# Low parts of the first MLP product's weights in blocks 1 to 3: a subtraction on VectorE replaced by a negated copy and an adding DMA

## The chip, the cores and the metric

One Trainium2 chip, one of its cores. The program runs on that core alone. The metric is the device time of one execution in microseconds: the median of three runs before the change is 722.54 us (721.73 to 723.35).

## What is computed

One layer of a decoder trunk on a sequence of 512 tokens of width 1024, all in float32: a norm, three token mixers side by side (stick-breaking attention, causal pooling, chunked gating), an output projection, and then a dense MLP with squared ReLU. The change concerns the MLP alone. Cut to it, the reference is:

```python
h = rms_norm(x, g_ff_pre[l])
ff = jnp.square(jax.nn.relu(h @ w_ff_in[l])) @ w_ff_out[l]
x = x + rms_norm(ff, g_ff_post[l])
```

`h` is 512x1024, `w_ff_in` 1024x4096, `w_ff_out` 4096x1024.

## The kernel before

**Split products.** Every float32 operand of a matmul is split into two float32r tiles, a high part `hi` (the value copied to float32r) and a low part `lo` (the value less `hi`). A product of two split operands is three matmuls, high by high, high by low and low by high (`mm3`, line 265). In the first MLP product the order on TensorE is weights' high by activations' high, weights' high by activations' low, weights' low by activations' high, so that the low part of the weights is wanted third in each k-step.

**Weights.** All weight matrices pass through one plan of chunks (`plan`, lines 112 to 175), each 128 partitions by 1024 values, 512 KB. `load_chunk` (line 179) issues the load of the next chunk on SP into one of three `raw` buffers. `split_chunk` (line 188) makes `whi` and `wlo`, of which there are six each: a copy on ScalarE into `whi`, and a subtraction raw minus `whi` on VectorE into `wlo`. Then it issues the load of the next chunk, which takes the raw buffer that is free first. A chunk of the first MLP product is four k-tiles of 256 columns, so that each of its 512 rows is 1 KB in memory. `Weights.ready` (line 243) makes chunks up to three ahead of the one in use (`AHEAD`), as far as six buffers allow.

**The MLP.** It runs in four blocks (`b`, line 949) of 1024 hidden columns. Each block has the first product, eight tiles `f` of 128 hidden columns (`ff_in`, line 874; 8 k-steps of three matmuls each), and the second product in four stages, `s2`, `s1`, `s3`, `s4` (lines 1010 to 1068), a scheme of half-size products in which VectorE also forms sums of weight blocks (`block_sums`, line 217). The first product of a block uses eight chunks, in pairs: the first of a pair has the first four k-steps, the second the other four, and both serve two tiles `f`. So the second chunk of a pair is wanted first four k-steps after the first. `ff_act` (line 890) takes each finished tile from PSUM, applies ReLU and square on ScalarE, forms sums on VectorE and splits them, for the second product only.

**Order.** TensorE and SP keep the order of the program (`InOrder`, line 80). For ScalarE and VectorE that order is switched off in the MLP (line 971), and the compiler's scheduler orders them by its own estimate. In the MLP after the first block's beginning, POOL has no work until the norm at the end.

Of the kernel before, what the change touches and what calls it, by code (L numbers as in the profile page):

```python
# [13 lines left out]
AF = mybir.ActivationFunctionType  # L14
ALU = mybir.AluOpType
# [33 lines left out]
def trunk_layer(ctx: ExitStack, tc: tile.TileContext, x, w_in, w_pool, pool_scale, gm_gain,  # L49
                w_spatial, b_spatial, w_br_sb, w_br_pool, w_br_gm, w_out, g_mix_pre,  # L50
                g_mix_post, g_ff_pre, g_ff_post, w_ff_in, w_ff_out, out):
    nc = tc.nc
# [45 lines left out]
    pe, act, dve, sp = (InOrder(e, True) for e in (nc.tensor, nc.scalar, nc.vector, nc.sync))  # L98
# [13 lines left out]
    plan = []  # L112

    derive = {}

    def plan_cols(w, c0, n=256):

        first = len(plan)
        for k in range(0, w.shape[1], CHUNK // n):
            plan.append([w[:, k:k + CHUNK // n, c0:c0 + n]])  # L120
        return range(first, len(plan))

    use = {}
    use["v"] = plan_cols(w_in_k, C_V, 512)

    def plan_qk(hp):
# [3 lines left out]

    plan_qk(0)
    use["u"] = plan_cols(w_in_k, C_U)
    use["gv"] = plan_cols(w_in_k, C_GV)
    plan_qk(1)
    use["p"] = plan_cols(w_in_k, C_P)
# [24 lines left out]
    for b in range(NB):  # L160
        for f in range(0, FT, 2):
            use["f1", b, f] = plan_cols(ff_in_k, (b * FT + f) * P)


        for stage in ("s2", "s1", "s3", "s4"):
            use[stage, b] = range(len(plan), len(plan) + (2 if stage == "s2" else FT // 2))
            for m in range(0, FT // 2, 2 if stage == "s2" else 1):
                b11, b12, b21, b22 = (
                    ff_out_k[:, b * FT + 2 * m + o:b * FT + 2 * m + o + 1, c:c + 512]
                    for o in range(2) for c in (0, 512))  # L170
                if stage == "s2":
                    plan.append([ff_out_k[:, b * FT + 2 * m + 1:b * FT + 2 * m + 4:2, :512]])
                else:
                    plan.append({"s1": [b11, b12], "s3": [b22, b12], "s4": [b22, b21]}[stage])
                    derive[len(plan) - 1] = (stage, m)

    loaded, made = [], []

    def load_chunk():
        raw = wp.tile([P, CHUNK], F32, name="raw", bufs=RAW)  # L180
        at = 0
        for v in plan[len(loaded)]:
            _, a, b = v.shape
            sp.dma_start(raw[:, at:at + a * b].rearrange("p (a b) -> p a b", a=a), v)
            at += a * b
        loaded.append(raw)

    def split_chunk(engines="v"):
        raw = loaded[len(made)]
        hi = wp.tile([P, CHUNK], F32R, name="whi", bufs=HL)  # L190
        lo = wp.tile([P, CHUNK], F32R, name="wlo", bufs=HL)
        if len(made) in derive:
            pieces = block_sums(raw, *derive[len(made)])
        else:
            pieces = [raw[:, n * CHUNK // len(engines):(n + 1) * CHUNK // len(engines)]
                      for n in range(len(engines))]
        at = 0
        for n, piece in enumerate(pieces):
            c = slice(at, at + piece.shape[1])
            at = c.stop  # L200
            e = engines[n % len(engines)]
            act.copy(hi[:, c], piece)
            (nc.gpsimd if e == "p" else dve).tensor_sub(lo[:, c], piece, hi[:, c].bitcast(F32))
        at = 0
        outs = []
        for v in plan[len(made)]:
            _, a, b = v.shape
            outs.append(tuple(t[:, at:at + a * b].rearrange("p (a b) -> p a b", a=a)
                              for t in (hi, lo)))
            at += a * b  # L210
        made.append(outs)
        if len(loaded) < len(plan):
            load_chunk()
# [3 lines left out]
    def block_sums(raw, stage, m):  # L217

        one, two = raw[:, :512], raw[:, 512:]
        if stage == "s1":  # L220
            t1s[m] = ff.tile([P, T], F32, name="t1", bufs=4)
            dve.tensor_add(t1s[m], one, two)
            return [one, t1s[m]]
        if stage == "s3":

            dve.tensor_add(t1s[m], t1s[m], one)
            dve.tensor_add(two, two, one)
            return [t1s[m], two]
        dve.tensor_add(two, two, t1s[m])
        return [raw]  # L230

    class Weights:
# [10 lines left out]
        def ready(self, i):  # L243
            live = self.chunks.start if self.keep else i
            while len(made) < min(len(plan), i + 1 + self.ahead, live + HL):
                split_chunk()
# [124 lines left out]
    if True:  # L371
# [32 lines left out]
        for step in V_ORDER.split():  # L404
            what = step.rstrip("0123")
            t, g = ([int(c) for c in step[len(what):]] + [0, 0])[:2]
            if what == "sq":
                if g == 0:
                    two[t] = sm.tile([P, 2], F32, name="n2")
                square_sum(xts[t][g], two[t][:, g:g + 1])  # L410
            elif what == "rms":
                rs[t] = rstd_d(two[t], "n")
            elif what == "scale":
                hns[t, g] = scaled(xts[t], rs[t], gpre, g)
            elif what == "turn":
                pts[t, g] = transposed(hns[t, g], bank("z", "trx"))
            elif what == "cols":
                split_to(hT, pts[t, g], t, g)
            elif what.startswith("split"):
                split_chunk(what[len("split"):])  # L420
            else:
                for which in {"hh": (0,), "rest": (1,), "mm": (0, 1)}[what]:
                    v_part(t, g, which)
# [432 lines left out]
    def between(t, k):  # L856

        if k == 2 and t >= 2:
            turn(t - 2)
        if k == 2 and t == 3:  # L860
            split_chunk("pp")
            later["ssq"] = residual(2, later["r"])
# [235 lines left out]
```

## Time and profile before

| | |
|---|---|
| runs, us | 721.73, 723.35, 722.54 |
| the profiled execution's own time, us | 722.87 |
| its span, first to last instruction, us | 721.1 |
| granted TensorE clock over the span | 0.996 of full speed |
| first products of blocks 1, 2 and 3, us from the span's start | 464.4 to 507.9, 546.15 to 589.7, 628 to 671.5 |
| DMA traffic | 89.80 MB, mean 125 GB/s |

The span counts from the first to the last instruction of one profiled execution; its own time includes what lies around it. A stage is named by the stretch of the span in which TensorE works on it. TensorE's matmuls are pipelined: one begins every 0.227 us, though each is shown as 0.39 us long.

### The profile page before, as it was taken

How to read it: one execution, taken by the hardware profiler on the slowest of the kernel's cores; microseconds unless marked ns; L12 is line 12 of the kernel's file. 1: busy time of each engine (PE TensorE's matmuls, PEld its weight loads, DVE VectorE, ACT ScalarE, POOL GpSimd, SP SyncE). 2: the span in 40 equal slices, each digit the busy share in tenths (PEclk: the TensorE clock that was granted, in tenths of full speed). 3: DMA queues.
4: the chain of work that ended last, by engine and by line, in shares of the span. 5: the costliest groups of instructions: out<-in, count | busy, mean ns of one | idle time of the engine just before them, and what ended most of it. 6: DMA issues, size and time to landing. Idle time of an engine off the chain costs nothing.

```text
span 721.1 us, 9135 instructions
## 1 busy us (share of the span) xinstructions
PE 698.6 (97%) x3320; PEld 576.7 (80%) x3320; DVE 494.0 (68%) x771; ACT 353.9 (49%) x593; POOL 54.0 (7%) x106
## 2 busy tenths in 40 slices
PE   7999999999999999999999998999999999999994
PEld 4889887788888888888889777888888888888774
DVE  6745799777777544243576776747885679757897
ACT  6566666655444333321445654555534553445541
POOL 4100222111121000000040000000000000000001
PEclk9999999999999999999999999999999999999998
DMA  8272312322325233262325235633356234643543
GB/s 278 80 207 84 115 60 60 90 68 70 96 59 146 89 90 114 74 220 87 116 89 176 99 106 175 181 113 115 119 165 208 92 117 148 188 133 116 162 160 117
DMA packets 72432, 89.80 MB, mean 125 GB/s; under 512 B 4546, under 2 KB 49730, under 8 KB 72387
## 3 DMA queue, kind: packets, MB, share of 16 engines
q1 hardware_dynamic: 72384, 89.21, 39.5%
q8 instruction: 26, 0.43, 0.2%
q14 instruction: 20, 0.16, 0.1%
q10 hardware_dynamic: 2, 0.00, 0.0%
HBM read 85.01 MB, written 4.19 MB: 124 GB/s over the span
## 4 chain that ended last, share of the span: by engine, by line
PE 80%; DVE 10%; DMA 4%; ACT 3%; issue 2%; POOL 1%; SPq 0%; POOLq 0%; DVEq 0%; ACTq 0%
PE psc L90 25%; PE accf L90 18%; PE accx L90 7%; PE psb L90 6%; PE acc L90 6%; PE accz L90 5%; PE accy L90 4%; PE psv L90 3%; DMA raw<-in_w_ff_out_dram 3%; DVE wlo L90 2%; DVE ys L90 2%; PE psgv L90 2%; PE z L90 1%; PE av L90 1%; PE pt L90 1%
## 5 line engine op out<-in xcount | busy, mean ns | idle before, releaser
L90 DVE TENSOR_TENSOR wlo<-raw,whi 128x1024 fp32r<-128x1024 f32 (+1 forms) x145 | 158.1, 1095 | 109.6 <-ACT whi L90 108.8
L90 ACT CAST whi<-raw 128x1024 fp32r<-128x1024 f32 (+1 forms) x152 | 139.4, 927 | 140.5 <-PE psc L90 31.0
L90 PE MATMUL psc<-hT,whi 128*128 128x512 f32 x576 | 182.2, 398 | 0.0
L90 PE MATMUL accf<-hT,whi 128*128 128x512 f32 x448 | 138.1, 390 | 1.4 <-ACT rl L90 1.4
L90 PEld LDWEIGHTS psc<-hT,whi 128*128 128x128 f32 x576 | 103.9, 188 | 21.0 <-issue 1.5
L90 PE MATMUL psc<-hT,wlo 128*128 128x512 f32 x288 | 112.6, 391 | 0.0
L90 PEld LDWEIGHTS accf<-hT,whi 128*128 128x128 f32 x448 | 84.0, 188 | 19.1 <-ACT rl L90 1.8
L90 PE MATMUL accf<-hT,wlo 128*128 128x512 f32 x224 | 87.2, 389 | 0.0
L90 PEld LDWEIGHTS psc<-hT,wlo 128*128 128x128 f32 x288 | 54.1, 188 | 11.6
L90 PEld LDWEIGHTS accf<-hT,wlo 128*128 128x128 f32 x224 | 42.1, 188 | 8.8
L90 ACT CAST ah<-ec 128x768 fp32r<-128x768 f32 (+1 forms) x32 | 30.2, 944 | 32.6 <-DVE ec L90 32.1
L90 PE MATMUL accx<-whi,ah 128*128 128x512 f32 x96 | 37.9, 394 | 2.9 <-DVE ys L90 2.9
L284 POOL TENSOR_TENSOR pr<-pv,mhalf 128x1 f32<-128x1 f32 x8 | 4.8, 605 | 470.7 <-DVE pv L90 470.7
L90 DVE TENSOR_TENSOR al<-ec,ah 128x768 fp32r<-128x768 f32 (+1 forms) x32 | 34.8, 1087 | 4.7 <-ACT ah L90 4.5
L90 PE MATMUL accx<-wlo,ah 128*128 128x512 f32 x96 | 37.4, 390 | 0.0
L90 PE MATMUL accx<-whi,al 128*128 128x512 f32 x96 | 37.4, 390 | 0.0
L90 DVE TENSOR_TENSOR_SCAN nb<-nb,zeros 128x128 f32<-128x128 f32 (+3 forms) x32 | 27.5, 863 | 7.5 <-POOL nb L482 7.1
L90 DVE TENSOR_TENSOR ec<-ec 128x256 f32<-128x256 f32 x64 | 26.7, 421 | 7.0 <-ACT ec L90 6.7
L90 ACT CAST whi<-t 128x512 fp32r<-128x512 f32 x32 | 19.7, 616 | 14.8 <-DVE t L90 9.2
L90 PE MATMUL accy<-whi,al 128*128 128x512 f32 (+1 forms) x64 | 24.7, 386 | 1.9 <-DVE al L90 1.9
L90 ACT CAST a<-pt 128x128 fp32r<-128x128 f32 (+3 forms) x32 | 13.6, 426 | 25.9 <-PE pt L90 25.8
L90 ACT ACTIVATE sg<-psc 128x512 f32<-128x512 f32 x24 | 14.3, 598 | 22.7 <-PE psc L90 22.7
(197 smaller groups left out, 1236.0 us busy)
## 6 DMA issues: line engine op xcount, KB each, us to landing
raw<-in_w_ff_out_dram SPq DMA_DIRECT2D x96, 256.0 KB, 3.2
raw<-in_w_in_dram SPq DMA_DIRECT2D x42, 512.0 KB, 3.8
raw<-in_w_ff_in_dram SPq DMA_DIRECT2D x32, 512.0 KB, 3.9
xt<-in_x_dram SPq DMA_DIRECT2D x16, 256.0 KB, 6.3
raw<-in_w_out_dram SPq DMA_DIRECT2D x8, 512.0 KB, 3.7
raw<-in_w_ff_out_dram SPq DMA_DIRECT2D x8, 512.0 KB, 3.8
raw<-in_w_br_sb_dram SPq DMA_DIRECT2D x4, 512.0 KB, 3.4
x1d<-xt SPq DMA_DIRECT2D x8, 256.0 KB, 2.7
```

The costliest lines, as they stand in the source:

```text
L90: i = op(*args, **kw).ins
L284: nc.gpsimd.tensor_tensor(r, v, mhalf, ALU.pow)
```

## The change

For the chunks of the first MLP product in blocks 1, 2 and 3 (`summed`, 8 chunks in each, 24 in all), `split_chunk` makes the low part in another way. ScalarE copies raw into `whi`, as before, and then copies raw times -1 into `wlo`. GpSimd's queue (POOL) then issues a DMA that reads the same chunk of `w_ff_in` from memory once more and adds it to what stands in `wlo`. VectorE has no part in these chunks. Block 0 and all other weights are made as before.

```diff
+    summed = set()
+
...
             use["f1", b, f] = plan_cols(ff_in_k, (b * FT + f) * P)
+            if b:
+                summed.update(use["f1", b, f])
...
         hi = wp.tile([P, CHUNK], F32R, name="whi", bufs=HL)
         lo = wp.tile([P, CHUNK], F32R, name="wlo", bufs=HL)
-        if len(made) in derive:
+        if len(made) in summed:
+            act.copy(hi, raw)
+            act.activation(lo, raw, AF.Copy, scale=-1.0)
+            v, = plan[len(made)]
+            _, a, b = v.shape
+            nc.gpsimd.dma_start(lo.rearrange("p (a b) -> p a b", a=a), v, accum_op=ALU.add)
+            pieces = []
+        elif len(made) in derive:
             pieces = block_sums(raw, *derive[len(made)])
```

How the instructions stand. On ScalarE at the head of block 1, in the last stage of block 0's second product (`ys` is the running output, `whi` and `wlo` the parts of weight chunks, `rl` and `ec` the ReLU and square of the first finished tile), the kernel before has:

```order
L90 CAST whi<-raw 128x1024
L90 ACTIVATE ys<-accx 128x512
L90 CAST whi<-raw 128x1024 x2
L90 ACTIVATE ys<-accx 128x512
L90 CAST whi<-raw 128x1024 x5
L90 ACTIVATE rl<-accf 128x512
```

and the changed one has, in the same place:

```order
L90 CAST whi<-raw 128x1024
L90 ACTIVATE ys<-accx 128x512
L90 CAST whi<-raw 128x1024 x2
L90 ACTIVATE wlo<-raw 128x1024
L90 ACTIVATE ys<-accx 128x512
L90 CAST whi<-raw 128x1024
L90 ACTIVATE wlo<-raw 128x1024
L90 CAST whi<-raw 128x1024
L90 ACTIVATE wlo<-raw 128x1024
L90 CAST whi<-raw 128x1024
L90 ACTIVATE wlo<-raw 128x1024
L90 CAST whi<-raw 128x1024
```

The second of the pair of CASTs is the first chunk of block 1; each first-product chunk now has a negated copy behind its CAST.

On VectorE at the same place (`accx`, `accy` and `accz` are PSUM tiles of the second product, `al` the low part of the activation sums), before:

```order
L90 TENSOR_TENSOR ys<-ys,accx 128x512
L90 TENSOR_TENSOR wlo<-raw,whi 128x1024 x5
L90 TENSOR_TENSOR ys<-ys,accz 128x512 x2
L90 TENSOR_TENSOR wlo<-raw,whi 128x1024
L90 TENSOR_TENSOR ys<-ys,accy 128x512 x2
L90 TENSOR_TENSOR wlo<-raw,whi 128x1024
L90 TENSOR_TENSOR ec<-ec 128x256
L90 TENSOR_TENSOR wlo<-raw,whi 128x1024 x2
L90 TENSOR_TENSOR ec<-ec 128x256 x2
L90 TENSOR_TENSOR al<-ec,ah 128x768
```

and after:

```order
L90 TENSOR_TENSOR ys<-ys,accx 128x512
L90 TENSOR_TENSOR wlo<-raw,whi 128x1024
L90 TENSOR_TENSOR ys<-ys,accz 128x512 x2
L90 TENSOR_TENSOR ys<-ys,accy 128x512 x2
L90 TENSOR_TENSOR ec<-ec 128x256 x3
L90 TENSOR_TENSOR al<-ec,ah 128x768
```

Eight subtractions are gone between these rows (four of the five, and the four behind them); the rest keeps its order.

On POOL, from the last norm before the MLP (`nr`) to the norms at the end (`pr`), the changed kernel has:

```order
L295 TENSOR_TENSOR pr<-pv,mhalf 128x1
L295 TENSOR_TENSOR nr<-nv,mhalf 128x1
L201 DMA wlo<-in_w_ff_in_dram 128x4x256 x24
L295 TENSOR_TENSOR pr<-pv,mhalf 128x1 x4
L1105 UNCONDITIONAL_BRANCH
```

The row of 24 transfers is new; before, the four `pr` stood right behind `nr`. TensorE's and SP's rows are the same in both kernels.

## Rows read from the trace of the kernel before

**Rows 1.** The page: span, and busy us (share) x instructions of each engine.

```profile
span 721.1 us, 9135 instructions
PE 698.6 (97%) x3320; PEld 576.7 (80%) x3320; DVE 494.0 (68%) x771; ACT 353.9 (49%) x593; POOL 54.0 (7%) x106
```

**Rows 2.** Stages: from:to, length, busy us of PE, PEld, DVE, ACT, POOL; clock; DMA.

```profile
546.15:589.70 43.55, 43.55 (x193) 36.09 (x193) 27.89 (x41) 23.05 (x33) 0.00 (x0) 1.00 0.37 122
...
671.50:690.00 18.50, 18.16 (x80) 14.72 (x80) 16.47 (x28) 9.78 (x18) 0.00 (x0) 1.00 0.62 213
690.00:721.00 31.00, 20.75 (x102) 16.99 (x100) 24.56 (x46) 8.63 (x18) 2.16 (x4) 0.91 0.28 106
```

**Rows 3.** PE's waits from 400 us: total us, times, longest.

```profile
PE accx L90 <- DVE ys L90: 2.9, 2, 2.0
PE accy L90 <- DVE al L90: 1.9, 2, 1.6
PE accf L90 <- ACT rl L90: 1.4, 1, 1.4
```

**Rows 4.** Timeline, last block, PE and DVE: start, length, engine, work [idle before].

```profile
694.85 0.50 PE L90 MATMUL accx<-whi,ah 128*128 128x512 f32 x1 [0.98 <-DVE ys L90]
...
674.82 0.69 DVE L90 TENSOR_TENSOR t<-t,raw 128x512 f32<-128x512 f32 x1 [1.58 <-DMA raw<-in_w_ff_out_dram]
```

**Rows 5.** Instruction groups from 380 us: count | busy us, mean ns | idle before.

```profile
L90 DVE TENSOR_TENSOR wlo<-raw,whi 128x1024 fp32r<-128x1024 f32 x52 | 63.2, 1222 | 35.8 <-ACT whi L90 35.6
L90 ACT CAST whi<-raw 128x1024 fp32r<-128x1024 f32 x52 | 54.1, 1051 | 78.1 <-DMA raw<-in_w_ff_in_dram 20.6 <-PE accf L90 17.4 <-PE accx L90 16.9
```

**Rows 6.** Timeline of ACT at the heads of blocks 1, 2 and 3.

```profile
453.00 1.99 ACT L90 CAST whi<-raw 128x1024 fp32r<-128x1024 f32 x2
...
457.69 1.05 ACT L90 CAST whi<-raw 128x1024 fp32r<-128x1024 f32 x1 [2.21 <-DMA raw<-in_w_ff_in_dram]
...
533.31 2.95 ACT L90 CAST whi<-raw 128x1024 fp32r<-128x1024 f32 x3 [4.61 <-PE accx L90]
539.48 1.05 ACT L90 CAST whi<-raw 128x1024 fp32r<-128x1024 f32 x1 [3.22 <-DMA raw<-in_w_ff_in_dram]
...
615.12 2.95 ACT L90 CAST whi<-raw 128x1024 fp32r<-128x1024 f32 x3 [4.65 <-PE accx L90]
621.24 1.05 ACT L90 CAST whi<-raw 128x1024 fp32r<-128x1024 f32 x1 [3.17 <-DMA raw<-in_w_ff_in_dram]
```

**Rows 7.** Timeline of PE: low-part matmuls at the heads of blocks 1, 2 and 3.

```profile
464.68 0.39 PE L90 MATMUL accf<-hT,wlo 128*128 128x512 f32 x1
...
546.44 0.39 PE L90 MATMUL accf<-hT,wlo 128*128 128x512 f32 x1
...
549.16 0.39 PE L90 MATMUL accf<-hT,wlo 128*128 128x512 f32 x1
...
628.25 0.39 PE L90 MATMUL accf<-hT,wlo 128*128 128x512 f32 x1
```

**Rows 8.** Loads of first-product chunks: SP issue, ns min/median/max; time to landing.

```profile
L90 SPq DMA_DIRECT2D raw<-in_w_ff_in_dram x32: 367/368/384, 328.6 to 630.0; - x32
...
DMA to landing us min/median/max: 3.6/3.9/5.2
```

**Rows 9.** DMA busy tenths and GB/s, 538 to 543 us, in 40 slices.

```profile
DMA  9999994179114992699999999999999999997238
GB/s 385 393 393 377 360 361 156 33 131 74 41 25 49 106 90 57 205 344 385 369 393 393 369 377 385 377 377 393 393 393 377 385 393 385 385 369 254 74 57 147
```

**Rows 10.** Stages of 5 us at the head of block 2; last columns DMA share, GB/s.

```profile
538.00:543.00 5.00, 5.00 (x23) 4.15 (x23) 2.31 (x2) 2.10 (x2) 0.00 (x0) 1.00 0.86 275
543.00:548.00 5.00, 5.00 (x23) 4.13 (x23) 4.87 (x6) 2.10 (x2) 0.00 (x0) 1.00 0.80 223
548.00:553.00 5.00, 5.00 (x23) 4.13 (x22) 2.42 (x4) 2.28 (x3) 0.00 (x0) 1.00 0.81 248
```

**Rows 11.** Chain of waits, 360 to 380 us: start, length, engine and work.

```profile
369.56 3.00 POOL wlo L203 x2
```

## The prediction

> **What bounds the kernel now.** I read the page's busy times first. TensorE (PE) is busy 698.6 of 721.1 us, VectorE (DVE) 494.0, ScalarE (ACT) 353.9 [rows 1]. So the reader should ask only one thing of any part of the change: does PE start a matmul sooner or later. Next I cut the span into stages. In the first product of the third MLP block (546.15 to 589.70 us) PE is busy all 43.55 us; only in the last stages, from 671.5 us on, does it have gaps [rows 2]. The waits of PE from 400 us to the end confirm it: three kinds, 2.9, 1.9 and 1.4 us, none of them on the weights of the first product [rows 3]. Of the gaps that DVE causes, the one behind the last changed block is 0.98 us, at 694.85 us [rows 4]. In the stages that the change touches there is nothing to win: PE has no gap there that a faster DVE could close.
>
> **What the change removes.** In blocks 1 to 3 it takes 24 subtractions of 128x1024 from DVE, at 1222 ns each, 29.3 us in all [rows 5]. They lie beside matmuls, so the gain on the path is 0. A gain later, through DVE's queue, would have to be carried from about 640 us to the crowded stretch from 671.5 us on, and it is not: at 674.82 us DVE stands idle for 1.58 us, waiting for a load of second-product weights [rows 4]. What DVE saves before that point is spent in such waits. I count 0.
>
> **What it adds on ACT.** 24 negated copies of 128x1024. No row shows this instruction; the nearest is the CAST of the same tile, 1051 ns [rows 5]. In a stage of 43.55 us ACT works 23.05 us [rows 2]; eight more copies make it 31.5. That fits, and the squared-ReLU work that they push back by a microsecond feeds only the second product or a PSUM bank that has a second one beside it. Cost by itself: 0. But each copy stands ahead of the adding transfer in the chain that makes a low part, so it counts below.
>
> **What it adds on POOL and the DMA engines.** 24 adding transfers of 512 KB. The low part that DVE made 1.2 us after its CAST now comes out of: CAST, negated copy, transfer. The question is whether it lands before PE wants it. POOL's queue has nothing else between the output projection and the last norm, and no load waits in it, so nothing is queued behind a transfer but the next one. SP's loads free their raw buffer at the end of the second ACT pass instead of DVE's, at about the same time (541.6 against 541.8 us for the second chunk, by rows 6 and the 1222 ns).
>
> **The windows.** In the middle of a stage a chunk has some 16 us of cover: PE uses one in 5.44 us (43.55 us for eight [rows 2]) and the code makes them three ahead. At the head of a block it has far less. There the buffers come free only as the block before ends, and the raw chunks arrive one after another. Take the second boundary. The CAST of the first chunk is the third of a group that ends at 533.31 + 2.95 = 536.26; with one more copy 537.31 [rows 6]. PE's first matmul on its low part is at 546.44 [rows 7]: window 9.1 us. The second chunk's CAST starts at 539.48; with both passes it is through at 541.58; PE wants its low part at 549.16, four k-steps of 0.68 us after the first one's: window 7.6 us. The same at the other two boundaries: first chunk 456.04 to 464.68 (8.6) and 619.12 to 628.25 (9.1); second chunk 459.79 to 464.68 + 2.72 = 467.40 and 623.34 to 630.97 (7.6 each) [rows 6, 7]. The third chunk is wanted only 10.88 us after the first, when the burst of loads is over. So PE is held at each of three boundaries by the second chunk, for what the transfer takes beyond 7.6 us.
>
> **The price of an adding transfer.** No row shows one. The nearest is the plain load of the same chunk: 3.6 to 5.2 us from issue to landing, 3.9 in the middle [rows 8]. At their busiest the engines move 393 GB/s of such loads [rows 9], so 512 KB (0.524 MB) move in 1.33 us and 2.6 us of the 3.9 are fixed.
> - Low end: it costs as much as that load, 3.9 us. It can't be below, since it moves the same bytes from the same tensor and more.
> - Passes: the sum needs the bytes of the weights and the bytes already in the tile; two passes of 1.33 us, or three if the write back counts too (2.7 or 4.0 us). The Trainium skill, "Collectives: The Full Stack", section "The bandwidth ceiling: the fold count and why AG ≠ RS ≠ AR", says that an add in the DMA engines costs by its two source reads and not by the arithmetic; by that rule two passes, and no run here shows it.
> - Sharing: from 538 to 553 us the engines are 86, 80 and 81% busy with the raw loads [rows 10]. A transfer that takes turns with them needs about twice its own time: 5.3 us for two passes, 8.0 for three.
> - POOL's part: an SP issue takes 0.37 us [rows 8]. What POOL needs to set up 512 rows of 1 KB is in no row; low end 0 beyond SP's, high end the 3.0 us that POOL takes for a pass over such a tile in two halves [rows 11]. I take the middle, 1.5.
>
> So the ends are 3.9 us, and 2.6 + 8.0 + 3.0 = 13.6 us; between these far ends I take 2.6 + 5.3 + 1.5 = 9.4 us, because the sharing is what rows 10 show for just this stretch, and two passes are the least that an add can be. That is 1.8 us beyond the 7.6 us window. **Sum:** 3 x 1.8 = +5.4 us. The profiled execution took 722.87 us, 0.33 more than the median of the runs, 722.54; the sum gives 728.3 against the one and 727.9 against the other. The ends give 0 and 3 x 6.0 = +18, 722.5 to 740.5.
>
> **The rivals.**
> - No difference (722.5 us). A transfer under 8.1 us holds PE by less than 0.5 us a boundary, 1.4 us in all; that is 0.2% of the time, about what a measurement of this kernel can tell from no change. For it: the plain load at 3.9 us has 4 us of room, and the raw loads leave a pause of about 1.5 us in the same stretch, the low digits of rows 9. Against it: three loads and a transfer are in flight at once there. The Trainium skill, "DMA: Bandwidth & Descriptors", section "Anatomy of one DMA — SWDGE (gpsimd) path", fits a DMA from this queue as 2.0 us plus its bytes at 436 GB/s. By that page an estimate for 512 KB is 3.2 us, 4.4 if the second operand's bytes count, and the sum would be +0; no run here shows such a DMA.
> - The transfers become the bound. If POOL or the engines need more than 5.44 us for each, served one after another, a block can't be fed: eight transfers of T us begun at 537.3 end at 537.3 + 2.6 + 8T, and PE wants the eighth at 549.16 + 3 x 10.88 = 581.8. At T = 6.5 PE is late by 10 us a block, 753 us in all; at T = 8 it is 22 us a block, 788 us. For it: 512 short rows a transfer and no price for POOL. Against it: twice the mean plain load's moving time is far below 5.44.
> - Faster. Freed of 24 subtractions, DVE enters the crowded stretch of the last block ahead of its present times, the 0.98 us wait at 694.85 us goes, and the drain behind it starts sooner by as much again: about 2 us, 720.5 us. From 671.5 us DVE works 16.47 of 18.5 us [rows 2], which speaks for it; the idle wait at 674.82 us for a load [rows 4] speaks against it, as DVE can't carry a lead across it. It decides only if the loads of the second product come earlier too, and the adding transfers rather push them back.
>
> That the change doesn't do what it says is no rival: the order shows 24 of each instruction gone and come, and every other row in its place.
>
> **How the numbers follow.** Transfers late at the three block heads, +1.4 to +18 us: 0.51, most likely +5.4, so 727.9 us. No difference: 0.31. Transfers the bound: 0.13. Faster: 0.05. Faster by over 0.2% is thus 0.05, within 0.2% 0.31, slower by over 0.2% 0.51 + 0.13 = 0.64. The range starts at the lowest run shown, 721.7, to hold the case of no difference, and ends at the high end of the forecast, 741; left out are the third and fourth case, 0.18. The likeliest case alone would be 724 to 741.
>
> **What would show it.** DVE's group of 128x1024 subtractions loses 24 and ACT gains 24 passes near 1.05 us. The view of DMA issues shows 24 transfers of 512 KB from POOL; their landing time is the whole question: near 9 us is my case, under 8 the first rival, and spacing above 5.44 us the second. PE's waits should then name the transfer into the low part, once or twice a block, within 4 us of the first product's start at about 464, 546 and 628 us plus what is already lost, and nowhere else. Wrong would be: no such wait; waits in the middle of a stage; or longer DVE instructions or raw loads that hold PE in the second product.

## The result and the profile after

The changed kernel takes 754.55 us (median of four runs, 753.32 to 758.40) against 722.94 us in the runs of the kernel before that stood beside it. That is a ratio of 1.0441, with a 95% interval of 1.0393 to 1.0489. It is 31.6 us slower where +5.4 was forecast, and it lies outside the range, which ended at 741. The profiled execution took 753.32 us.

The page of the changed kernel, to be laid beside [rows 1]: span, busy times, POOL's DMA queue q0 (packets, MB, share of 16 engines) and two kinds of transfer (count, KB each, median us to landing).

```profile
span 751.3 us, 9194 instructions
PE 709.6 (94%) x3320; PEld 580.0 (77%) x3320; DVE 464.8 (62%) x747; ACT 374.7 (50%) x617; POOL 85.6 (11%) x130
...
q0 software_dynamic: 12672, 12.58, 10.4%
...
raw<-in_w_ff_in_dram SPq DMA_DIRECT2D x32, 512.0 KB, 6.1
wlo<-in_w_ff_in_dram POOLq DMA_DIRECT2D x24, 512.0 KB, 11.8
```

DVE has lost 29 us, ACT has gained 21, and neither of them sets the time. The two groups that are new are ACT's negated copy and POOL's issue of the transfer (count, busy us, mean ns):

```profile
L201 POOL DMA_DIRECT2D wlo<-in_w_ff_in_dram x24 | 30.7, 1280 | 257.3 <-ACT wlo L90 180.4 <-PE accy L90 73.8 <-ACT rl L90 3.1
...
L90 ACT ACTIVATE wlo<-raw 128x1024 fp32r<-128x1024 f32 x24 | 25.3, 1053 | 0.0
```

The line to look at is q0. It has nothing but the 24 transfers, and they take 10.4% of 16 engines' span: 0.104 x 751.3 / 24 = 3.26 us of all 16 engines for each. The same sum can be made for q1, the queue of SP's transfers, which are the plain loads and a few others. On the page of the kernel before it has 0.395 x 721.1 us for 89.21 MB, so 1.67 us for a chunk of 0.524 MB:

```profile
q1 hardware_dynamic: 72384, 89.21, 39.5%
```

An add takes nearly twice that. (At the 393 GB/s of [rows 9], the rate of the densest slices, a chunk would move in 1.33 us.)

The waits from 400 us to the end (total us, times, longest), against [rows 3]. First a line of the kernel before, then the changed one:

```profile
DVE t L90 <- DMA raw<-in_w_ff_out_dram: 17.9, 20, 2.2
```

```profile
DVE t L90 <- DMA raw<-in_w_ff_out_dram: 42.0, 17, 4.6
...
ACT whi L90 <- DMA raw<-in_w_ff_in_dram: 37.5, 18, 4.4
...
PE accf L90 <- ACT rl L90: 10.4, 7, 2.2
...
PE accf L90 <- DMA wlo<-in_w_ff_in_dram: 7.4, 6, 1.4
...
PE accy L90 <- DVE al L90: 7.0, 4, 2.6
```

The forecast wait is there, PE for the transfer into the low part, 7.4 us. But PE waits longer for ScalarE's ReLU (10.4 us, 1.4 before), and `al` is 5.1 us up, 0.5 of it in block 0, before any transfer. The first two rows say where that comes from: DVE and ACT themselves stand for **raw loads**, 42.0 and 37.5 us, where it was 17.9 and 20.6 before (20.6 is in [rows 5]).

**Where the 30 us lie.** I cut both spans at the first matmul of each product. First the kernel before, then the changed one (columns as in [rows 2]; the second last is the DMA share, the third last the granted clock):

```profile
507.75:545.98 38.23, 38.23 (x169) 31.48 (x168) 32.69 (x46) 17.11 (x23) 0.00 (x0) 1.00 0.53 164
...
671.32:721.10 49.78, 39.09 (x181) 31.89 (x179) 41.03 (x73) 18.59 (x36) 2.16 (x4) 0.94 0.41 146
```

```profile
463.26:513.22 49.96, 44.66 (x194) 35.74 (x193) 20.39 (x33) 25.93 (x36) 6.36 (x5) 1.00 0.85 191
513.22:554.05 40.83, 38.65 (x169) 31.37 (x168) 30.65 (x47) 19.94 (x27) 3.82 (x3) 1.00 0.55 154
554.05:605.71 51.66, 46.32 (x194) 36.85 (x192) 20.73 (x34) 27.57 (x38) 6.37 (x5) 0.97 0.82 184
...
698.31:751.30 52.99, 40.39 (x181) 32.95 (x179) 41.14 (x74) 18.68 (x36) 2.19 (x4) 0.90 0.41 147
```

The three first products are longer by 6.44, 8.14 and 8.84 us (43.52 each before), 23.4 in all. The three second products, the last one with the end of the kernel, are longer by 2.60, 1.94 and 3.21 (38.23, 38.30 and 49.78 before), 7.8 in all. Block 1 starts 1.0 us sooner. Together that is the 30.2 us between the spans.

PE's timeline shows the pauses inside block 1 (idle us before the row, and who ended it):

```profile
465.12 0.47 PE L90 MATMUL accf<-hT,wlo 128*128 128x512 f32 x1 [1.25 <-DMA wlo<-in_w_ff_in_dram]
...
469.47 0.47 PE L90 MATMUL accf<-hT,wlo 128*128 128x512 f32 x1 [1.35 <-DMA wlo<-in_w_ff_in_dram]
...
483.42 0.72 PE L90 MATMUL accf<-hT,whi 128*128 128x512 f32 x2 [0.56 <-ACT rl L90]
...
502.20 0.73 PE L90 MATMUL accf<-hT,whi 128*128 128x512 f32 x2 [2.15 <-ACT rl L90]
...
520.74 0.50 PE L90 MATMUL accy<-whi,al 128*128 128x512 f32 x1 [1.47 <-DVE al L90]
```

Blocks 2 and 3 repeat the pattern: 1.13 and 1.36 for the low parts, 0.67 and 2.18 for the ReLU; then 0.93 and 1.40, 1.63 and 2.11. So of the 23.4 us in the first products the low parts hold 7.42 and the ReLU 9.30. In two of them the clock is 0.97, worth 0.03 x 52 = 1.6 us each. The rest, 3.6 us over 12 pauses, is 0.3 for each: an idle time counts from a modelled end 0.16 us after the next matmul could have begun, and the first matmul behind a pause is slower.

**Why the ReLU is late.** ACT's timeline at the head of block 1, against [rows 6]:

```profile
453.92 1.05 ACT L90 ACTIVATE wlo<-raw 128x1024 fp32r<-128x1024 f32 x1
...
457.60 1.06 ACT L90 ACTIVATE wlo<-raw 128x1024 fp32r<-128x1024 f32 x1
...
461.60 1.05 ACT L90 CAST whi<-raw 128x1024 fp32r<-128x1024 f32 x1
...
468.01 1.04 ACT L90 CAST whi<-raw 128x1024 fp32r<-128x1024 f32 x1 [4.40 <-DMA raw<-in_w_ff_in_dram]
...
472.38 1.05 ACT L90 CAST whi<-raw 128x1024 fp32r<-128x1024 f32 x1 [2.37 <-DMA raw<-in_w_ff_in_dram]
...
481.82 1.05 ACT L90 CAST whi<-raw 128x1024 fp32r<-128x1024 f32 x1 [2.34 <-DMA raw<-in_w_ff_in_dram]
482.78 0.59 ACT L90 ACTIVATE rl<-accf 128x512 f32<-128x512 f32 x1
...
500.60 1.04 ACT L90 CAST ah<-ec 128x1024 fp32r<-128x1024 f32 x1 [7.41 <-DVE ec L90]
501.55 0.59 ACT L90 ACTIVATE rl<-accf 128x512 f32<-128x512 f32 x1
```

From 468 us on the CASTs come 4.3 to 5.1 us apart (there is one at 477.48 that is not shown). The three with a wait start at the moment their raw load lands, and the ReLU at 482.78 stands in ACT's queue behind one of them; PE goes on at 483.42. The second, longer pause has one more link. The ReLU at 501.55 stands behind the copy `ah`, that waits for DVE's `ec`, and DVE's queue stood before that for loads of second-product weights, 4.51 and 2.03 us:

```profile
491.54 0.69 DVE L90 TENSOR_TENSOR t<-raw 128x512 f32<-128x512 f32 x1 [4.51 <-DMA raw<-in_w_ff_out_dram]
...
498.34 0.69 DVE L90 TENSOR_TENSOR t<-raw 128x512 f32<-128x512 f32 x1 [2.03 <-DMA raw<-in_w_ff_out_dram]
...
500.15 0.42 DVE L90 TENSOR_TENSOR ec<-ec 128x256 f32<-128x256 f32 x1
```

**Why the loads are late.** One of seven stretches of 5 us at the head of block 1, to be read against [rows 10]:

```profile
470.00:475.00 5.00, 5.00 (x24) 4.13 (x23) 0.00 (x0) 2.60 (x5) 1.35 (x2) 1.00 1.17 238
```

Before, the engines were 80 to 86% busy in such a stretch. Now the share stands at 1.15 to 1.18 for 30 us (it adds up the time of every packet, and here more packet time is counted than 16 engines have), and what moves is 232 to 271 GB/s, 238 in the row shown. A raw load and an adding transfer are 1.05 MB; at 238 GB/s a pair takes 4.4 us, about the spacing of the CASTs. From 380 us on, the median raw load of this matrix lands 8.3 us after its issue; it was 3.9 [rows 8]. The 96 loads of second-product weights of 256 KB land hardly later by the median, 3.5 us against 3.2 (the eight of 512 KB: 8.0 against 3.8). So DVE's longer waits for them come from single loads that meet the transfers and from loads that are issued later because the queues run late; the runs don't split the two.

### The profile page after: what moved, and what is told of

Same layout as the page of the kernel before. It is cut to its first block, busy times and chain, and to the rows that moved or that the text cites. A ratio compares the mean times of both kernels' runs of the same rounds, so it can differ in the third digit from the quotient of the medians.

```text
span 751.3 us, 9194 instructions
## 1 busy us (share of the span) xinstructions
PE 709.6 (94%) x3320; PEld 580.0 (77%) x3320; DVE 464.8 (62%) x747; ACT 374.7 (50%) x617; POOL 85.6 (11%) x130
## 3 DMA queue, kind: packets, MB, share of 16 engines
q1 hardware_dynamic: 72384, 89.21, 38.2%
q0 software_dynamic: 12672, 12.58, 10.4%
## 4 chain that ended last, share of the span: by engine, by line
PE 56%; DMA 17%; DVE 16%; ACT 6%; issue 3%; SPq 1%; POOL 0%; DVEq 0%; POOLq 0%; ACTq 0%
PE psc L90 24%; DMA raw<-in_w_ff_out_dram 8%; DMA raw<-in_w_ff_in_dram 7%; PE psb L90 6%; PE accx L90 5%; PE acc L90 5%; DVE wlo L90 3%; PE psv L90 3%; PE accz L90 2%; ACT whi L90 2%; DVE al L90 2%; DVE t L90 2%; DVE ys L90 2%; PE accf L90 2%; PE psf L90 2%
## 5 line engine op out<-in xcount | busy, mean ns | idle before, releaser
L90 ACT CAST whi<-raw 128x1024 fp32r<-128x1024 f32 (+1 forms) x152 | 138.8, 925 | 129.5 <-DMA raw<-in_w_ff_in_dram 37.5
L90 DVE TENSOR_TENSOR wlo<-raw,whi 128x1024 fp32r<-128x1024 f32 (+1 forms) x121 | 128.8, 1069 | 68.6 <-ACT whi L90 67.6
L90 PE MATMUL accf<-hT,whi 128*128 128x512 f32 x448 | 141.3, 397 | 10.4 <-ACT rl L90 10.4
L90 PE MATMUL accf<-hT,wlo 128*128 128x512 f32 x224 | 89.0, 397 | 7.4 <-DMA wlo<-in_w_ff_in_dram 7.4
L201 POOL DMA_DIRECT2D wlo<-in_w_ff_in_dram x24 | 30.7, 1280 | 257.3 <-ACT wlo L90 180.4
L90 ACT CAST ah<-ec 128x768 fp32r<-128x768 f32 (+1 forms) x32 | 30.2, 943 | 56.8 <-DVE ec L90 56.3
L90 DVE TENSOR_TENSOR t<-raw 128x512 f32<-128x512 f32 x16 | 11.1, 691 | 30.4 <-DMA raw<-in_w_ff_out_dram 30.4
L493 POOL TENSOR_SCALAR_AFFINE_SELECT nb<-nb 128x128 f32<-128x128 f32 x32 | 15.6, 487 | 117.6 <-ACT nb L90 100.3
## 6 DMA issues: line engine op xcount, KB each, us to landing
wlo<-in_w_ff_in_dram POOLq DMA_DIRECT2D x24, 512.0 KB, 11.8
```

What stands on the lines that cost most here:

```text
L90: i = op(*args, **kw).ins
L201: nc.gpsimd.dma_start(lo.rearrange("p (a b) -> p a b", a=a), v, accum_op=ALU.add)
L493: nc.gpsimd.affine_select(tile_[:, n - P:n], tile_[:, n - P:n], [[-1, P]], ALU.is_ge, fill, base=-1, channel_multiplier=1)
```

## The experiments

Each edit is made to the changed kernel, and each ratio is to runs of the kernel before that stood beside it.

**1. Does PE lose by waiting for the low parts?**

```diff
-                              for t in (hi, lo)))
+                              for t in (hi, hi if len(made) in summed else lo)))
```

> The changed kernel, but TensorE reads the high part of the 24 chunks a second time in place of their low part (so their low parts are left out of the sum); copies and adding transfers go on as before, and nothing waits for a transfer's landing but the next writer of the same buffer. Theory A (the transfers slow the raw loads, and ScalarE's queue and the second product's loads fall behind those): most of the loss stays, 742 to 750 us, with the waits for the ReLU and for the sums' low parts still there; only the 7.4 us of waits for the transfer itself go. Rival B (the late low part is what holds TensorE, and the other waits only follow from it): 722 to 728 us.

Measured: 759.32 us, ratio 1.0497 [1.0456, 1.0539]. PE's waits:

```profile
PE accf L90 <- ACT rl L90: 16.1, 4, 5.3
PE accy L90 <- DVE al L90: 8.5, 3, 3.7
```

The wait on the transfers is gone and the time is no better; it is above the 742 to 750 us expected too. The raw loads still land late, after 9.4 us (median from 380 us on), and ACT waits 35.5 us for them, 24.1 ahead of CASTs and 11.4 ahead of negated copies. So the late low parts alone don't make the loss; with them out of the way it comes in through the ReLU and the sums. One reserve: the scheduler gave ACT's copies another order here, so the size of the ReLU's share is this kernel's own.

**2. The same transfers without the add.**

```diff
-            nc.gpsimd.dma_start(lo.rearrange("p (a b) -> p a b", a=a), v, accum_op=ALU.add)
+            nc.gpsimd.dma_start(lo.rearrange("p (a b) -> p a b", a=a), v)
```

> The changed kernel with the same 24 transfers from the same queue, but copying instead of adding (so the low part is left out and the weights themselves stand in its place). Theory A with two or more passes for an add: a copy takes less of the engines, spans of both loads sharing are shorter, landing about 6 to 8 us instead of 11.8, time 725 to 735 us. Rival C (the price is that of POOL's queue and of 512 more rows read from memory, not of the adding): landing 10 to 12 us and 748 us or more.

Measured: 727.58 us (722.54 to 731.10, ten runs), ratio 1.0053 [1.0019, 1.0087]. POOL's queue and the landing times on the page, then the busiest of three stretches of 5 us at the head of block 2:

```profile
q0 software_dynamic: 12672, 12.58, 6.7%
...
raw<-in_w_ff_in_dram SPq DMA_DIRECT2D x32, 512.0 KB, 5.1
wlo<-in_w_ff_in_dram POOLq DMA_DIRECT2D x24, 512.0 KB, 7.1
```

```profile
543.00:548.00 5.00, 5.00 (x24) 4.14 (x23) 2.73 (x4) 4.34 (x5) 0.88 (x2) 1.00 1.12 343
```

These are as many packets and bytes from the same queue, with the same passes on ACT, and the loss falls from 4.4% to 0.5%. The instructions on ACT and DVE stand in the same order in both kernels, by operation, tile and shape. In the profiled execution, of 723.65 us, all three first products take 43.52 us again, and PE waits neither for the low parts nor more than 1.2 us for the ReLU. The engines give up to 343 GB/s here and gave 238 with the add. A copy costs 0.067 x 721.6 / 24 = 2.01 us of all engines, an add 3.26. So the add is what separates the two kernels. It has two prices: its time on the DMA engines, and POOL's issue, 1.28 us against 0.75 for a copy. No run takes them apart, but POOL is busy only 1.35 of the 5 us of the row at 470 us, so the half microsecond more can't be what holds the engines at 238 GB/s.

**3. The extra pass on ACT, and DVE's relief, each by itself.** First the negated copy is kept and DVE's subtraction put behind it, with no transfer:

```diff
-            v, = plan[len(made)]
-            _, a, b = v.shape
-            nc.gpsimd.dma_start(lo.rearrange("p (a b) -> p a b", a=a), v, accum_op=ALU.add)
+            dve.tensor_sub(lo, raw, hi.bitcast(F32))
```

> The changed kernel without its 24 transfers: ScalarE still makes the negated copy, VectorE then writes the low part over it by subtraction as in the kernel before. Theory A: 722 to 724 us, the extra copy costs nothing. Rival D (the extra pass in ScalarE's queue delays the ReLU that frees PSUM): 728 us or more, with waits of TensorE for the ReLU.

Measured: 723.53 us, ratio 0.9999 [0.9978, 1.0020]. Then the subtraction runs on POOL, with no extra copy and no transfer:

```diff
-            act.activation(lo, raw, AF.Copy, scale=-1.0)
-            v, = plan[len(made)]
-            _, a, b = v.shape
-            nc.gpsimd.dma_start(lo.rearrange("p (a b) -> p a b", a=a), v, accum_op=ALU.add)
+            nc.gpsimd.tensor_sub(lo, raw, hi.bitcast(F32))
```

> The low parts of the 24 chunks by a subtraction on POOL (about 2.6 us each by the 1.29 us for half a tile), no copy on ScalarE and no transfer: VectorE is relieved of the same 24 subtractions and no byte is moved more. Theory A and the prediction's term for the relief: 722 to 724 us, no gain. Rival E (relief of VectorE is worth something in the last stages): 719 to 721 us.

Measured: 723.72 us, ratio 0.9989 [0.9964, 1.0013]. 24 more passes on ACT cost nothing, and 24 fewer on DVE bring nothing. The relief is not the whole 29 us here: DVE is busy 476.7 us in the profiled execution (729.07 us), 17 less than before, since some of its other instructions take longer beside POOL's. The two terms that the prediction put at 0 are 0 as far as these runs can tell.

**4. Which transfers cost.** The condition on the chunks is narrowed: the first two of each block, chunks 2 and 3, the last four, and the last one alone.

```diff
-            if b:
+            if b and f == 0:
```

> Adding transfers only for the first two chunks of each block (6), the two with the windows of 8.6 to 9.1 and 7.6 us. Prediction's own case: they land 1 to 3 us late and nothing else happens, 725 to 732 us, with waits of TensorE for the transfer. Theory A beyond it: the raw loads of the next chunks land later too, but the backlog is only two transfers deep and is worked off within the stage, so no waits for the ReLU. Rival F: 6 x 1.3 = +8, 731 us, so this run tells by its waits, not its time.

Measured: 735.59 us, ratio 1.0161 [1.0127, 1.0194]. PE's pauses at the head of block 1, and the clock behind the longer one:

```profile
465.70 0.47 PE L90 MATMUL accf<-hT,wlo 128*128 128x512 f32 x1 [0.85 <-DMA wlo<-in_w_ff_in_dram]
...
471.36 0.76 PE L90 MATMUL accf<-hT,wlo 128*128 128x512 f32 x1 [2.67 <-DMA wlo<-in_w_ff_in_dram]
```

```profile
471.00:475.00 4.00, 3.65 (x9) 2.90 (x10) 2.39 (x3) 1.04 (x1) 0.00 (x0) 0.50 0.73 220
```

This is the forecast mechanism nearly alone: six transfers, landing after 10.2 us, and pauses at the three heads of 8.75 us in all (1.43 and 1.42 at the second, 0.93 and 1.45 at the third; the view puts the one of 1.42 down to ACT's `whi`, the other five to the transfers). After a pause of 2.67 us PE ran at the lower of its two levels, 1.2 GHz (clock 0.50), for some microseconds; with a mean of 0.93 over 49.7 us that is another 3.5. Pauses and clock together bring the time above the 725 to 732 us expected. The wait on the ReLU stays at 1.2 us (1.4 before the change).

```diff
-            if b:
+            if b and f == 2:
```

> The change only for chunks 2 and 3 of each of blocks 1 to 3 (6 transfers in all). The first two alone cost 11.8 us against the kernel before, the last four 6.4, all eight 31.6. Theory A (transfers and the loads of the burst share saturated engines, so what is lost depends on how many transfers meet the burst): chunks 2 and 3 alone, whose low parts are wanted 10.9 us after the first, cost 1 to 6 us, waits on rl under 3 us in all, the transfers land in 8 to 10 us; the three parts then add up to 19 to 24 us, short of 31.6, and the rest comes from all of them together. Rival (each transfer has a price of its own, whatever goes beside it): the rest of the sum, 31.6 - 11.8 - 6.4 = 13.4 us, so 736 to 738 us.

Measured: 724.35 us, ratio 1.0004 [0.9986, 1.0023]; waits on the ReLU 1.1 us, transfers landing after 11.8 us. That is no loss at all, below the 1 to 6 us that I had expected; the transfers were later than the 8 to 10 us expected too, and PE never waits for them. A price for each transfer, the rival, is out: six of them cost 1.6% or nothing, by their place.

```diff
-            if b:
+            if b and f >= FT // 2:
```

> Adding transfers only for the last four chunks of each of the three blocks (12 instead of 24); the first four get their low parts from VectorE. Theory A (the loss comes from the crowding at the block head, where the raw loads come in a burst): the burst is untouched, 722 to 728 us, a raw load lands in about 4 us at the head. Rival F (a transfer costs the same wherever it stands, 31.6 us over 24 = 1.3 us each): 12 x 1.3 = +16, 738 us.

Measured: 729.90 us, ratio 1.0088 [1.0056, 1.0119], above the 722 to 728 us expected. All first products take 43.52 us, and the median raw load lands after 3.9 us, as expected. The transfers land after 8.9 us. What is lost lies later, the largest piece at 683.21 us in the last block, 3.45 us for `al` (0.34 before). In block 0, before any transfer, `ys` holds PE for 2.51 us, where it was 1.97. DVE's waits for second-product loads, against the 17.9 us before:

```profile
DVE t L90 <- DMA raw<-in_w_ff_out_dram: 38.1, 17, 5.3
```

By operation, tile and shape ACT and DVE keep the order of the kernel before, but for the 12 subtractions gone and the 12 copies come, and the extra copies cost nothing by themselves (experiment 3). So most of the 0.9% is left to the transfers, by way of late loads in DVE's queue, as in the changed kernel, which has the same pause (2.58 us at 706.95). It is not a direct meeting: DVE stood 4.34 us for a load until 680.32, and the last transfer, issued at 643.82, had landed by 655.6. By then the lag was carried on in the queues.

```diff
-            if b:
-                summed.update(use["f1", b, f])
+            if b and f == FT - 2:
+                summed.update(use["f1", b, f][1:])
```

> One adding transfer a block, for its last chunk (3 in all), wanted some 24 us after it is issued. Theory A: 722 to 724 us, and the landing time is that of a transfer with little beside it: 2.6 us fixed plus about 3.3 us of moving plus 1.3 us of issue, about 7 us. Rival C (POOL's side sets the price): 10 us or more even so.

Measured: 724.53 us, ratio 1.0007 [0.9984, 1.0030]. Slightly above the 722 to 724 us expected, and no different from the kernel before. Three transfers, with only the usual loads beside them:

```profile
DMA to landing us min/median/max: 6.4/6.6/7.9
```

The three parts of the set cost 1.6, 0.0 and 0.9%, 2.5% together, and the changed kernel loses 4.4%. So far as the parts add up, the remaining 1.9%, some 14 us, exist only when all eight transfers of a block run one after another beside the loads.

**5. Is it the second read from memory?** The transfer adds the raw tile, which is on the chip, in 128 rows of 4 KB instead of 512 of 1 KB.

```diff
-            v, = plan[len(made)]
-            _, a, b = v.shape
-            nc.gpsimd.dma_start(lo.rearrange("p (a b) -> p a b", a=a), v, accum_op=ALU.add)
+            nc.gpsimd.dma_start(lo, raw, accum_op=ALU.add)
```

> The changed kernel, but the 24 transfers add from the raw tile on chip (128 rows of 4 KB) instead of from memory (512 rows of 1 KB); a raw buffer is then free only when its transfer has landed. Theory A with the price by row: less engine time than 3.3 us a transfer and combined rate above 238 GB/s, but three raw buffers held longer, 725 to 745 us. Rival G (the price is by byte of the add, or the held buffers outweigh it): 750 us or more.

Measured: 759.09 us, ratio 1.0484 [1.0450, 1.0518], in rival G's range.

```profile
q0 software_dynamic: 3456, 12.58, 9.5%
...
wlo<-raw POOLq DMA_DIRECT2D x24, 512.0 KB, 5.8
```

```profile
ACT whi L90 <- DMA raw<-in_w_ff_in_dram: 49.7, 19, 7.2
...
PE accf L90 <- ACT rl L90: 16.2, 7, 4.6
```

With no second read from memory and a quarter of the packets an add takes 0.095 x 756.2 / 24 = 2.99 us of all engines, hardly less than 3.26. So the engine time of an add comes neither from that read nor from the short rows. It lands sooner (5.8 us), but now it holds one of the three raw buffers until it has been read, and ACT waits 49.7 us for raw loads. The time is no test of the saturation, since loads are late for a second reason here; the 2.99 us is what the run is for.

**6. Is ScalarE's queue the way by which late loads reach PE?** Both copies move to DVE.

```diff
-            act.copy(hi, raw)
-            act.activation(lo, raw, AF.Copy, scale=-1.0)
+            dve.tensor_copy(hi, raw)
+            dve.tensor_scalar_mul(lo, raw, -1.0)
```

> The changed kernel with both copies of its 24 chunks (the high part and the negated one) made on VectorE instead of ScalarE, so that no ReLU stands behind a copy that waits for a raw load; transfers and loads stay. Theory A (saturated DMA engines make raw loads late, and 10.4 us of the loss reach TensorE only because the ReLU queues behind the waiting copy on ScalarE): the waits of accf on rl fall from 10.4 to under 3 us, the transfers still land after 10 us or more and the waits of accf on wlo stay near 7 us, raw loads still take 7 to 9 us; the time falls to 738 to 748 us, unless the same queueing turns up on VectorE, where the copies then stand ahead of the sums and al for the second product: then the waits of accy on al rise above 7 us by what the ReLU lost. Rival B (ScalarE's 24 extra passes are what delays the ReLU, apart from the loads): the waits on rl go and nothing takes their place, near 735 us. Rival C (the ReLU is late because TensorE itself is late): nothing changes, 751 to 758 us with the waits on rl still near 10.

Measured: 749.45 us, ratio 1.0355 [1.0333, 1.0378].

```profile
PE accf L90 <- DMA wlo<-in_w_ff_in_dram: 9.4, 3, 4.1
PE accy L90 <- DVE al L90: 7.9, 4, 3.7
...
PE accf L90 <- ACT rl L90: 1.1, 1, 1.1
```

```profile
DVE whi L90 <- DMA raw<-in_w_ff_in_dram: 32.7, 15, 4.1
```

The ReLU's waits are back at 1.1 us, none of it in blocks 1 to 3, though the copies, now on DVE, still stand 32.7 us for raw loads (37.5 on ACT). So it was the queue and not PE's own lateness (rival C). Rival B asked for 735 us. But the loss only falls from 31.6 to 25.5 us: the transfers now land after 14.5 us, PE waits for them 2.25, 3.06 and 4.07 us, once at each head, and the mean clock of the three first products falls to 0.96, 0.96 and 0.93 (0.04 x 48 = 1.9 us in each of two, 0.07 x 50 = 3.5 in the third). The raw loads land in 4.9 us, not the 7 to 9 expected; PE loses more to the transfers and to the clock instead. The time is 1.5 us above the band that I gave.

## Why the prediction was wrong

**Right.** Nothing to win: relief of DVE was worth 0 (17 us of it in experiment 3), and the extra copies cost 0 by themselves, at 1053 ns against the 1051 taken. PE is held at each head by the low parts of the first two chunks, where the windows said. The windows of block 1 were 8.6 and 7.6 us. There the negated copies end at 454.97 and 458.66 us, and PE's first matmuls on these low parts start at 465.12 and 469.47, so the low parts came after 10.2 and 10.8 us. I had taken 9.4. By that figure the first chunk is late as well, by 0.3 to 0.8 us, which the text passes over; it held PE for 0.93 to 1.25 us. (A small slip in the reading: PE has gaps in block 0 too, not only from 671.5 us on; the three largest before that, 1.37, 1.56 and 1.97 us, lie from 411 to 443 us.) Three boundaries at 2.5 us are 7.4 us of idle time, where the sum has 5.4. POOL's issue took 1.28 us, not 1.5.

**Wrong: the sharing was priced on one side only.** The step reads "A transfer that takes turns with them needs about twice its own time", with the engines at 80 to 86% from raw loads. The factor of two was put on the transfer alone. The loads take turns as well, and of them the text says only that SP's loads free their buffers "at about the same time". The numbers for the other half stood in the prediction. An add was put at 2.7 us of moving time, one comes at least every 5.44 us and faster in the burst, and with one in 5 us 0.82 + 2.7 / 5 is 1.36 of what there is. By that sum the loads of the burst had to come late, not just the transfer. (A smaller excess is borne: with the plain copies it is 0.82 + 2.0 / 5 = 1.22, and little was lost.) That price was left out, and it is most of the loss: 9.3 us of pauses for the ReLU, 4.6 us of `al` behind the first transfer, and the clock that falls behind pauses. The prediction had seen the ReLU's way to PE and put it at 0, for a push of a microsecond and "a PSUM bank that has a second one beside it". That held for the extra copies alone (experiment 3), but not for an ACT queue that stands 2.3 to 7.4 us at a time. The Trainium skill, "DMA: Bandwidth & Descriptors", section "Issuing engines are not separate DMA queues", says that transfers run on the same 16 engines and interleave, whichever engine started them. The trace agrees: the loads of another queue went from 3.9 us to 8.3.

**The size of an add.** Two passes of 1.33 us, 2.7, were taken; 3.26 measured (2.99 from on-chip rows; 3.3 to 3.9 by the same sum in the runs with fewer transfers). That is 1.95 times the 1.67 us of a plain load, and 1.6 times the 2.01 us of a plain copy from POOL's queue. So two passes were about right against the load, and what was too small is the price of a pass. The Trainium skill, "Collectives: The Full Stack", section "The bandwidth ceiling: the fold count and why AG ≠ RS ≠ AR", has it that an add costs by its two source reads and not by the arithmetic. The trace is near that, 1.95 times the load, and less near it against the copy, 1.6; the runs don't tell reads from arithmetic. The estimate from "DMA: Bandwidth & Descriptors" in the Trainium skill, section "Anatomy of one DMA — SWDGE (gpsimd) path", 3.2 or 4.4 us to landing, does not hold here: 6.6 us with only the usual loads beside it, and 7.1 us for the plain copies of experiment 2.

**A rival whose number came out, for another reason.** The transfers as the bound gave 753 us at T = 6.5 us, close to 754.55. But it needs more than 5.44 us for each transfer, and a pair takes 4.4. PE is not fed too slowly in the middle of the block, as that case has it; it pauses at the head and, through ACT's and DVE's queues, behind late loads. I don't count that rival as confirmed. The rival with no difference fell with the transfer's 9.7 to 14.9 us to landing, and the faster one with experiment 3.

**The sign of wrong that was named.** "Waits in the middle of a stage" and "raw loads that hold PE in the second product" are both there, the second by way of DVE's `t` and `al` (a load until 517.58, PE at 520.74 us).

**What stays open.** Of the 14 us that only the whole set costs, the runs don't give each mechanism its share. They change places when one is taken out (experiments 1 and 6). How the lag of the last four chunks' kernel reaches the last block, when its transfers have landed, is not shown, and neither is where the spread of the plain copies' runs, 722.54 to 731.10, comes from.

No version here beats the kernel before: the best (no transfers, chunks 2 and 3 alone, or three transfers in all) can't be told from it.

## What to carry to other kernels

Before a transfer is added to a stretch whose DMA share is 80%, put its engine time on top of that share, and if the sum is well above 1, reprice the loads that are already there, not just the new transfer. Here 0.82 + 3.26 / 5 = 1.47 lost 4.4% and 0.82 + 2.01 / 5 = 1.22 lost 0.5%. Then follow each late load to the in-order queue in which its first reader stands, and ask what else is in that queue: here the ReLU that frees a PSUM bank. Work that is taken off an engine with slack buys nothing with which to pay.

## What the runs showed that was not expected

- An add in a DMA takes 1.6 times the engine time of the same copy (3.26 against 2.01 us for 512 KB in rows of 1 KB), and reading its source on the chip in rows of 4 KB saves little (2.99).
- Engines that are full of such transfers move 238 GB/s beside loads (share 1.17, over 5 us), where loads with plain copies gave 343 (share 1.12, over 5 us) and loads alone 275 (share 0.86, over 5 us [rows 10]) and 393 in the densest slices [rows 9].
- Behind some pauses PE ran at 1.2 GHz, the lower of its two levels. In block 2 of the changed kernel, in steps of 2 us:

```profile
591.00:593.00 2.00, 0.00 (x0) 0.00 (x0) 1.49 (x4) 1.53 (x2) 0.00 (x0) 1.00 0.00 0
593.00:595.00 2.00, 1.94 (x6) 1.61 (x7) 1.92 (x4) 1.97 (x5) 0.00 (x0) 0.73 0.00 0
595.00:597.00 2.00, 2.00 (x6) 1.51 (x6) 1.71 (x3) 1.94 (x5) 0.00 (x0) 0.50 0.41 131
```

PE does nothing from 591 to 593 us, and the clock falls when it is at work again; the row shows 6 matmuls in 2 us, then, where others at 1.00 show 10. The pause of 2.15 us in block 1 left the clock at 1.00, that of 2.18 us here did not, so the length of the pause alone does not decide it.
- With the subtractions on POOL, DVE's own of the same size took 1360 ns on the mean, 1222 before, and its `ec` 530, 421 before; it still cost nothing here.
